# Log sigmoid of the forget gates on GpSimd and ScalarE, places of their own for the extra tokens' values and the last probabilities

## The chip, the core and the metric

The kernel runs on one core of one Trainium2 chip. The time is that of one execution on the device in microseconds (us), median of several runs. The engines are named as the profile names them: PE is TensorE's matmul, PEld its weight load, DVE VectorE, ACT ScalarE, POOL GpSimd, SP the engine that issues the transfers (DMAs).

## What is computed

The reference is one layer of a hybrid decoder: 2048 prompt tokens and 16 meta tokens ahead of them, and 8 samples of 4 tokens that decode from caches. Every token is normalised and projected by one wide matrix; half of the width goes through an mLSTM with four heads, the other half through attention over a window of 128 tokens with sinks; both are gated, projected back to 1024 columns and normalised with the residual. What the change touches is the forget gate of the mLSTM:

```python
def mlstm_inputs(mq, mk, mv, mi, mf):
    ...
    log_i = mi.astype(f32)
    log_f = jax.nn.log_sigmoid(mf.astype(f32))

def mlstm_chunk(state, q, k, v, log_i, log_f):
    b = jnp.cumsum(log_f, axis=1)
    dmat = b[:, :, None, :] - b[:, None, :, :] + log_i[:, None, :, :]
    ...
    m_t = jnp.maximum(inter, jnp.max(dmat, axis=2))
    w = jnp.exp(dmat - m_t[:, :, None, :])
    qk = jnp.einsum('btsh,bshd->btsh', q, k) * w
```

The log sigmoid of f is min(f, 0) - log(1 + e), with e = exp(-|f|). The kernel takes the logarithm as 2 artanh(z) with z = e / (2 + e), by an odd polynomial in z up to z to the 13th.

## The kernel before

The prompt is cut into 16 chunks of 128 tokens, a token to a partition. Matrices are multiplied as two halves of 16 bits each (high and low), so that a projection of 512 columns takes 24 matmuls (`proj`, L298 to L301).

**Start (to about 90 us).** Weights come in pieces, are scaled and split (`prep`, L244 to L277: maxima of the arrived pieces at L261, the split on ACT at L259 and DVE at L276). The 48 extra tokens (32 of the samples, 16 meta tokens) and chunk 0 are projected as the weights come; matmuls at L307 and L308 are those of the extra tokens (tile `px`, evicted at L310 on ACT and at L311 and L317 on DVE). The extra tokens' gates (`ge`, L571) and those of chunk 0 (`gts`, L508) each call `log_sigmoid_rows`; PE transposes the result of the first at L574 and L575. Their values `ve` are written by L317 into the first 48 rows of `vaug[1]` (L546). There are two such buffers, `vaug[0]` and `vaug[1]`: chunk n's values go to `vaug[n % 2]` (L429 and L430), so chunk 1's use the one that holds `ve`. Column 128 of each head in them is 1, written once at the start (L222). Transposed extra tokens (`xef`) lie in the arena `ea`.

**Phase A (to about 515 us).** For each chunk n: the gates (`a_gate`: 16 small matmuls at L513 and L516, the sums on DVE at L518 and L519, then `log_sigmoid_rows` into `Gf[n % 2]`, its forget gates, and `Gi[n % 2]`, its input gates); projections q, k, v and o (evicted by DVE at L433 or L430, two PSUM buffers `pj`; for q and k also L437 on ACT and L438 on DVE); the mLSTM of the chunk, which begins with transposes of Gf and Gi on PE (L749, L750). On POOL run in this phase the products of the queries (L792, behind a transposing DMA into `qT`, and L793) and small powers (L327, L499). Between these steps stand jobs of the samples and the preparation of further weights. The log sigmoid is a chain of small operations of 4 elements a partition in the tile `ls`: 13 on DVE from L472 to L483 with ACT's exponential (L473) among them, and a copy of the input gates (L484), which hangs on nothing else of the chain. It runs 17 times: for the extra tokens and for 16 chunks.

**Phase B (from about 515 us).** For each chunk the attention: projections, then four units of two heads (`s_unit`, L1256: scores on PE at L1271, maxima on DVE at L1272, exponentials on ACT at L1278, the probabilities split into the two halves of `hl` by ACT at L1279 and DVE at L1280, for the meta tokens into `mhl` by ACT at L1283 and POOL at L1284). Units 0 and 1 share one tile `hl`, units 2 and 3 the next; there is one buffer of it, and a transposing DMA reads each pair into a tile from `stg`. The meta tokens' part is transposed in `s_sums` (`mT`), and PE multiplies probabilities and values in `s_pv` (L1313 for meta tokens, L1324 for the window). The output projection is at L1351, and the layer norm follows (on DVE, and on POOL at L340, L1181 and L1182). The last chunk, 15, is written out by hand at the end of the program.

**Order.** The steps are written one after the other in the program, and the framework's scheduler puts each engine's instructions into an order of its own, by its estimate of when each is ready. In that order each engine then works strictly. All transfers are issued by SP, in the order of its queue.

Of the kernel before, what the change touches and what calls it, by code (L numbers as in the profile page):

```python
# [9 lines left out]
F16 = mybir.dt.float16  # L10
BF16 = mybir.dt.bfloat16
I32 = mybir.dt.int32
AF = mybir.ActivationFunctionType
ALU = mybir.AluOpType
AX = mybir.AxisListType

P = 128
D = 1024
KT = 8
NCH = 16  # L20
NM = 16
NS = 32
NE = NS + NM
H = 4
# [17 lines left out]
def tile_hymba_step(  # L42
# [7 lines left out]
    V, A, G, T, S = nc.vector, nc.scalar, nc.gpsimd, nc.tensor, nc.sync  # L50
# [4 lines left out]
    mn = ctx.enter_context(tc.tile_pool(name="mn", bufs=1))  # L55
# [9 lines left out]
    def pt(shape):  # L65
        return psum("pt", shape, 3)
# [7 lines left out]
    def small(tag, n, dt=F32, bufs=2):  # L74
        return sp.tile([P, n], dt, tag=tag, name=tag, bufs=bufs)
# [5 lines left out]
    def work(tag, shape, dt=F32, bufs=None):  # L81
        return mn.tile(shape, dt, tag=tag, name=tag, bufs=bufs or KB4.get(tag, 1))
# [23 lines left out]
    def dmat(out, in_):  # L106
        return dma(out, in_, S.dma_start_transpose)
# [107 lines left out]
    Gi = [cst.tile([P, P], F32, name=f"Gi{i}") for i in range(2)]  # L215
    vaug = [cst.tile([P, H, 129], F32, name=f"vaug{i}") for i in range(2)]
# [250 lines left out]
    def log_sigmoid_rows(gts, rows, buf):  # L467

        f = gts[:, 4:8]
        w = small("ls", 32)[:rows]  # L470
        na, e, d, r, z, z2, q = (w[:, 4 * i:4 * i + 4] for i in range(7))
        V.scalar_tensor_tensor(na, f, -1.0, f, op0=ALU.mult, op1=ALU.min)  # L472
        A.activation(e, na, AF.Exp)  # L473
        V.tensor_scalar(d, e, 2.0, None, op0=ALU.add)
        V.reciprocal(r, d)
        V.tensor_tensor(z, e, r, op=ALU.mult)
        V.tensor_tensor(z2, z, z, op=ALU.mult)
        V.tensor_scalar(q, z2, 1.0 / 13, None, op0=ALU.mult)
        for c in (11, 9, 7, 5, 3):
            V.scalar_tensor_tensor(q, q, 1.0 / c, z2, op0=ALU.add, op1=ALU.mult)  # L480
        V.scalar_tensor_tensor(q, q, 1.0, z, op0=ALU.add, op1=ALU.mult)
        V.tensor_scalar(d, f, 0.0, None, op0=ALU.min)
        V.scalar_tensor_tensor(Gf[buf][:rows, 0:P:32], q, -2.0, d, op0=ALU.mult, op1=ALU.add)  # L483
        V.tensor_copy(Gi[buf][:rows, 0:P:32], gts[:, 0:4])  # L484

    def head_stats(g, nh, dd, rows):

# [14 lines left out]
    def a_gate(n):  # L502
        c = ca[n]
        gts = small("gts", 8)
        if n == 0:
            ps = po([P, 8])
            proj32(ps, lambda k: tg[:, k])
            V.tensor_tensor(gts, ps, bg, op=ALU.add)  # L508
            log_sigmoid_rows(gts, P, 0)
            return  # L510
        ps = pt([P, 16])
        for k in range(KT):
            T.matmul(ps, c.xT[:, k, :], wg.t[:, k].rearrange("p c n -> p (c n)"), start=(k == 0), stop=False,  # L513
                     skip_group_check=True)
        for k in range(KT):
            T.matmul(ps[:, 0:8], c.xT[:, KT + k, :], wg.t[:, k, 0], start=False, stop=(k == KT - 1),  # L516
                     skip_group_check=True)
        V.scalar_tensor_tensor(gts, ps[:, 8:16], wg.ev, bg, op0=ALU.mult, op1=ALU.add)  # L518
        V.scalar_tensor_tensor(gts, ps[:, 0:8], wg.ev, gts, op0=ALU.mult, op1=ALU.add)  # L519
        log_sigmoid_rows(gts, P, n % 2)  # L520
# [15 lines left out]
    def e_arena():  # L536
        return Arena(mn.tile([P, 2048], F32, tag="wkv", name="ea"))

    E = St()
    ea = e_arena()  # L540
# [2 lines left out]
    qe = work("qs", [P, 512])[:NE]  # L543
    ke = work("At", [P, 512])[:NE]
    oe = work("g", [P, 512])[:NE]
    ve = vaug[1][:NE]  # L546

    sto = stage(512, "w")
    load(sto, w_a[3])
# [9 lines left out]
    hl = work("hl", [P, 2, D], F16)  # L559
    ln0_(xe, NE, hl.rearrange("p c d -> p (c d)").bitcast(BF16)[:NE])  # L560
    split_e(EE[:, 0], xe, NE, s_x)
    dmat(ET, EE[:, 0])
    xef = ea.take(8 * NE).rearrange("p (k t) -> p k t", t=NE)
    ps = pt([P, 8, NE])
    for j in range(8):
        T.transpose(ps[:, j], xe[:, j * P:(j + 1) * P], ident[:NE, :NE])
# [2 lines left out]
    for k in range(KT):  # L569
        T.matmul(ps[:NE], xef[:, k], tg[:, k], start=(k == 0), stop=(k == KT - 1))  # L570
    V.tensor_tensor(ge, ps[:NE], bg[:NE], op=ALU.add)  # L571
    log_sigmoid_rows(ge, NE, 1)
    pr = pt([P, 2, P])
    T.transpose(pr[:, 0, :NE], Gf[1][:NE, :], ident[:NE, :NE])  # L574
# [3 lines left out]
    rows = ea.take(3 * NE).rearrange("p (c t) -> p c t", t=NE)  # L578
# [27 lines left out]
                    op=ALU.subtract)  # L606
# [40 lines left out]
    for j in range(2):  # L647
        ps = po([P, 2, 256])
        for i in range(2):
            h = 2 * j + i  # L650
# [605 lines left out]
    def s_unit(n, u):  # L1256

        c = cb[n]
        pvc = cb.get(n - 1)
        lo = 0 if pvc is not None else P  # L1260
        if u % 2 == 0:
            c.hl = work("hl", [P, 2, 4, 256], F16)
        hl, q, h0 = c.hl, u % 2, 2 * u
        mxs, nb, sums = c.mxs, c.nb, c.sums
        mask = swamask[:, c.half, lo:]
        p = work(("g", "SI")[u % 2], [P, 2, NW])
        for i in range(2):
            h = h0 + i
            ps = pt([P, NW])
            for x in range(2):  # L1270
                T.matmul(ps[:, lo:], c.qT[:, h], kTs[:, 2 * (h // 4) + x, lo:], start=(x == 0), stop=(x == 1))  # L1271
            V.tensor_tensor_reduce(p[:, i, lo:], ps[:, lo:], mask, sc_s, sink60[:, h:h + 1],  # L1272
                                   op0=ALU.add, op1=ALU.max, accum_out=mxs[:, h:h + 1])
        hs = slice(h0, h0 + 2)
        V.tensor_scalar(nb[:, hs], mxs[:, hs], -1.0, LN2x12, op0=ALU.mult, op1=ALU.add)  # L1275
        for i in range(2):
            h = h0 + i
            A.activation(p[:, i, lo:], p[:, i, lo:], AF.Exp, bias=nb[:, h:h + 1], accum_out=sums[:, h:h + 1])  # L1278
        A.activation(hl[:, 0, 2 * q:2 * q + 2, lo:], p[:, :, lo:2 * P], AF.Copy)  # L1279
        V.tensor_tensor(hl[:, 1, 2 * q:2 * q + 2, lo:], p[:, :, lo:2 * P], hl[:, 0, 2 * q:2 * q + 2, lo:],  # L1280
                        op=ALU.subtract)
        m = c.mhl[:, u // 2, :, 2 * q:2 * q + 2]
        A.activation(m[:, 0], p[:, :, 2 * P:], AF.Copy)  # L1283
        G.tensor_tensor(m[:, 1], p[:, :, 2 * P:], m[:, 0], op=ALU.subtract)  # L1284
        if lo:
            G.memset(hl[:, :, 2 * q:2 * q + 2, 0:P], 0.0)
        if q:
            pT = work("stg", [P, 2, 4, 2, P], F16)
            dmat(out=pT.rearrange("p c h e q -> p (c h e) q"),
                                  in_=hl.rearrange("p c h k -> p (c h k)"))  # L1290
            c.PT.append(pT)
# [88 lines left out]
    for n in range(NCH - 1):  # L1380
        b_load(n + 1)
        b_q(n)
        b_kv(n)
        if n > 0:
            s_pv(n - 1)
        b_az(n)
        if n == 2:
            b_out(0)
        s_start(n)
        s_unit(n, 0)  # L1390
        s_unit(n, 1)
        b_z(n)
        s_unit(n, 2)
        s_unit(n, 3)
        s_sums(n)
        if n == 0:
            z = work("xs", [P, D])[:NS]
            dma(z, ze_d)
            final(z, NS, y_s)
        elif 1 < n < NCH - 2:  # L1400
            b_out(n - 1)
            cb.pop(n - 2, None)

    n = NCH - 1
# [113 lines left out]
```

## Time and profile before

| | before |
|---|---|
| median of 3 runs | 1063.71 us (1061.87 to 1066.89) |
| profiled execution | 1059.23 us |
| its span on the core | 1057.4 us |
| granted TensorE clock, mean | 0.993 |
| PE busy | 1026.1 us, 97% of the span |
| DVE busy | 728.7 us, 69% |
| ACT busy | 441.3 us, 42% |
| POOL busy | 247.6 us, 23%, 270 instructions |

The page gives busy time by engine, then the span in 40 slices (a digit is the busy share in tenths; PEclk is the clock that TensorE was granted), then the chain of work that ended last. A row of a timeline reads: start, duration, engine, line, operation, what is written from what, with the shape, how often, and in brackets the idle time of the engine before it and what ended that. A row of the waits of an engine reads: the instruction's line, what it waited for, total us, how many times, the longest.

### The profile page before, as it was taken

What the parts mean: (1) busy time and instruction counts of PE and PEld (TensorE: products, weight loads), DVE (VectorE), ACT (ScalarE), POOL (GpSimd) and SP (SyncE); (2) the same over time, 40 slices, a digit from 0 to 9 for tenths busy, and PEclk for the clock granted to TensorE, in tenths of its full rate; (3) what the DMA queues carried; (4) which work ended last, traced back from release to release, by engine and by line L of the source; (5) the groups of instructions that cost most, each with busy time, mean ns of one, the idle gap of its engine ahead of it and who ended that gap; (6) DMA issues with size and microseconds to landing.
All of it is one profiled execution on the core that took longest, in us unless ns stands there. A gap on an engine that the chain in (4) does not pass through costs nothing.

```text
span 1057.4 us, 17650 instructions
## 1 busy us (share of the span) xinstructions
PE 1026.1 (97%) x6399; PEld 571.0 (54%) x6399; DVE 728.7 (69%) x2056; ACT 441.3 (42%) x1112; POOL 247.6 (23%) x270
## 2 busy tenths in 40 slices
PE   7998999999999999999999999999999999999996
PEld 3544666655556555555565555555555455555552
DVE  5996876767766887787557676656566566666674
ACT  5783333336244554552334334343334333343430
POOL 2101313211111001013111332233331233332322
PEclk9998999999999999999999999999999999999998
DMA  9946366464794775755866463555445555545452
GB/s 332 267 133 164 99 145 154 115 187 88 233 236 123 222 247 140 231 133 160 291 188 124 92 160 89 132 131 117 108 113 127 128 124 139 108 102 135 113 114 76
DMA packets 245809, 161.83 MB, mean 153 GB/s; under 512 B 207945, under 2 KB 220953, under 8 KB 244409
## 3 DMA queue, kind: packets, MB, share of 16 engines
q1 hardware_dynamic: 245722, 160.70, 58.3%
q8 instruction: 50, 0.82, 0.3%
q14 instruction: 37, 0.30, 0.1%
HBM read 68.22 MB, written 43.58 MB: 106 GB/s over the span
## 4 chain that ended last, share of the span: by engine, by line
PE 69%; DMA 11%; DVE 10%; ACT 6%; issue 3%; POOL 1%; SPq 1%; DVEq 0%; ACTq 0%
PE pj L1351 14%; PE pj L301 14%; PE pj L298 14%; PE pj L299 14%; DMA stg<-hl 3%; PE pt L1271 3%; PE po L1324 2%; DMA stg<-in_dram 1%; DMA xT<-hl 1%; DMA kT<-kh 1%; ACT w_o L259 1%; DMA wd_o<-w_o 1%; DVE w_o L276 1%; PE po L816 1%; PE po L817 1%
## 5 line engine op out<-in xcount | busy, mean ns | idle before, releaser
L301 PEld LDWEIGHTS <-xT 128*128 128x128 f16 x992 | 96.9, 98 | 98.2 <-issue 1.0
L299 PEld LDWEIGHTS <-xT 128*128 128x128 f16 x992 | 97.4, 98 | 96.7 <-issue 5.2
L298 PEld LDWEIGHTS <-xT 128*128 128x128 f16 x992 | 97.4, 98 | 94.1 <-issue 2.8
L1351 PEld LDWEIGHTS <-EE 128*128 128x128 f16 x720 | 70.3, 98 | 79.0
L1351 PE MATMUL pj<-wr_o,EE 128*128 128x512 f16 x360 | 82.3, 379 | 0.0
L1351 PE MATMUL pj<-w_o,EE 128*128 128x512 f16 x360 | 82.1, 379 | 0.0
L1278 ACT ACTIVATE SI<-SI,nb 128x272 f32<-128x272 f32 (+1 forms) x64 | 32.4, 507 | 66.0 <-DVE nb L1275 66.0
L298 PE MATMUL pj<-w_o,xT 128*128 128x512 f16 x120 | 46.9, 390 | 3.2 <-DVE vaug L430 3.2
L1278 ACT ACTIVATE g<-g,nb 128x272 f32<-128x272 f32 (+1 forms) x64 | 32.2, 503 | 42.4 <-DVE nb L1275 42.4
L1284 POOL TENSOR_TENSOR mhl<-SI,mhl 128x32 f16<-128x32 f32 x32 | 12.6, 395 | 157.6 <-ACT mhl L1283 157.6
L298 PE MATMUL pj<-wr_az,xT 128*128 128x512 f16 x128 | 48.5, 379 | 0.0
L299 PE MATMUL pj<-wr_z,xT 128*128 128x512 f16 x128 | 48.5, 379 | 0.0
L298 PE MATMUL pj<-wr_aq,xT 128*128 128x512 f16 x128 | 48.5, 379 | 0.0
L299 PE MATMUL pj<-wr_aq,xT 128*128 128x512 f16 x128 | 48.5, 379 | 0.0
L299 PE MATMUL pj<-wr_az,xT 128*128 128x512 f16 x128 | 48.5, 379 | 0.0
L298 PE MATMUL pj<-wr_z,xT 128*128 128x512 f16 x128 | 48.5, 379 | 0.0
L793 POOL TENSOR_TENSOR qs<-qs,SI 128x512 f32<-128x512 f32 x16 | 20.9, 1307 | 113.5 <-ACT SI L784 113.3
L299 PE MATMUL pj<-w_o,xT 128*128 128x512 f16 x120 | 46.7, 390 | 0.0
L1181 POOL TENSOR_TENSOR xs<-xs,gb 128x1024 f32<-128x1024 f32 (+1 forms) x16 | 42.8, 2674 | 15.4 <-DMA stg<-hl 9.3
L298 PE MATMUL pj<-w_v,xT 128*128 128x512 f16 x120 | 46.0, 383 | 0.0
L299 PE MATMUL pj<-w_v,xT 128*128 128x512 f16 x120 | 45.8, 382 | 0.0
L792 POOL TENSOR_TENSOR qs<-qT 128x512 f32<-128x512 f16 x16 | 20.2, 1260 | 109.2 <-DMA qT<-qh 58.9
(463 smaller groups left out, 2492.1 us busy)
## 6 DMA issues: line engine op xcount, KB each, us to landing
stg<-in_dram SPq DMA_DIRECT2D x28, 512.0 KB
xs<-in_dram SPq DMA_DIRECT2D x16, 512.0 KB
h_d<-xs SPq DMA_DIRECT2D x16, 512.0 KB
xT_d<-xT SPq DMA_DIRECT2D x16, 512.0 KB
xs<-h_d SPq DMA_DIRECT2D x16, 512.0 KB
xT<-xT_d SPq DMA_DIRECT2D x16, 512.0 KB
out_dram<-xs SPq DMA_DIRECT2D x15, 512.0 KB
hn_d<-g SPq DMA_DIRECT2D x16, 258.0 KB
```

What stands on the lines that cost most here:

```text
L259: A.activation(w.t[:, 2 * i:2 * i + 2, 0, :], s, AF.Abs, accum_out=mx4[:, i:i + 1])
L298: T.matmul(ps, xT[:, k, :], w.t[:, k, 0, :n], start=(k == 0), stop=False)
L299: T.matmul(ps, xT[:, k, :], w.t[:, k, 1, :n], start=False, stop=False)
L301: T.matmul(ps, xT[:, KT + k, :], w.t[:, k, 0, :n], start=False, stop=(k == KT - 1))
L792: G.tensor_tensor(c.qs, c.qT[:, 0], c.qT[:, 1], op=ALU.add)
L793: G.tensor_tensor(c.qs, c.qs, c.SI, op=ALU.mult)
L1181: G.tensor_tensor(z, z, lg[:rows], op=ALU.mult)
L1271: T.matmul(ps[:, lo:], c.qT[:, h], kTs[:, 2 * (h // 4) + x, lo:], start=(x == 0), stop=(x == 1))
L1278: A.activation(p[:, i, lo:], p[:, i, lo:], AF.Exp, bias=nb[:, h:h + 1], accum_out=sums[:, h:h + 1])
L1284: G.tensor_tensor(m[:, 1], p[:, :, 2 * P:], m[:, 0], op=ALU.subtract)
L1324: T.matmul(pso[:, h], l, r, start=False, stop=(i == len(last) - 1), skip_group_check=True)
L1351: T.matmul(ps, c.yT[:, a, :], w[:, k, t, :], start=(first and j == 0), stop=(last and j == len(mm) - 1))
```

## The change

Three things.

- `log_sigmoid_rows`: the exponent's argument is now |f|, by ACT's Abs, and the exponential takes it with scale -1. Of the thirteen DVE operations two stay there, the reciprocal and the last combination into Gf; the others run on POOL, as products and sums apart (a step of the polynomial that was one operation of DVE is two of POOL), and min(f, 0) is now half of f - |f|. With the copy of the input gates POOL has 18 operations in a call. The polynomial is the same.
- The extra tokens' values `ve` get a place of their own in the arena `ea`, with their ones column written there; to make room, `xef` moves to a tile `kw`.
- In chunk 15 the units 2 and 3 write their probabilities into a tile of their own, `hl2`, in the buffer that held the weights `wkv`.

Lines shift: what is L484 to L545 in the kernel before is 3 lines further down in the changed one, L546 to L1261 is 4 further, and what follows L1262 is 7 further.

```diff
@@ -469,19 +469,22 @@
         f = gts[:, 4:8]
         w = small("ls", 32)[:rows]
         na, e, d, r, z, z2, q = (w[:, 4 * i:4 * i + 4] for i in range(7))
-        V.scalar_tensor_tensor(na, f, -1.0, f, op0=ALU.mult, op1=ALU.min)
-        A.activation(e, na, AF.Exp)
-        V.tensor_scalar(d, e, 2.0, None, op0=ALU.add)
+
+        A.activation(na, f, AF.Abs)
+        A.activation(e, na, AF.Exp, scale=-1.0)
+        G.tensor_scalar(d, e, 2.0, None, op0=ALU.add)
         V.reciprocal(r, d)
-        V.tensor_tensor(z, e, r, op=ALU.mult)
-        V.tensor_tensor(z2, z, z, op=ALU.mult)
-        V.tensor_scalar(q, z2, 1.0 / 13, None, op0=ALU.mult)
-        for c in (11, 9, 7, 5, 3):
-            V.scalar_tensor_tensor(q, q, 1.0 / c, z2, op0=ALU.add, op1=ALU.mult)
-        V.scalar_tensor_tensor(q, q, 1.0, z, op0=ALU.add, op1=ALU.mult)
-        V.tensor_scalar(d, f, 0.0, None, op0=ALU.min)
+        G.tensor_tensor(z, e, r, op=ALU.mult)
+        G.tensor_tensor(z2, z, z, op=ALU.mult)
+        G.tensor_scalar(q, z2, 1.0 / 13, 1.0 / 11, op0=ALU.mult, op1=ALU.add)
+        for c in (9, 7, 5, 3, 1):
+            G.tensor_tensor(q, q, z2, op=ALU.mult)
+            G.tensor_scalar(q, q, 1.0 / c, None, op0=ALU.add)
+        G.tensor_tensor(q, q, z, op=ALU.mult)
+        G.tensor_tensor(d, f, na, op=ALU.subtract)
+        G.tensor_scalar(d, d, 0.5, None, op0=ALU.mult)
         V.scalar_tensor_tensor(Gf[buf][:rows, 0:P:32], q, -2.0, d, op0=ALU.mult, op1=ALU.add)
-        V.tensor_copy(Gi[buf][:rows, 0:P:32], gts[:, 0:4])
+        G.tensor_copy(Gi[buf][:rows, 0:P:32], gts[:, 0:4])
 
     def head_stats(g, nh, dd, rows):
 
@@ -543,7 +546,8 @@
     qe = work("qs", [P, 512])[:NE]
     ke = work("At", [P, 512])[:NE]
     oe = work("g", [P, 512])[:NE]
-    ve = vaug[1][:NE]
+    ve = ea.take(H * 129).rearrange("p (h d) -> p h d", d=129)[:NE]
+    G.memset(ve[:, :, 128:129], 1.0)
 
     sto = stage(512, "w")
     load(sto, w_a[3])
@@ -560,7 +564,7 @@
     ln0_(xe, NE, hl.rearrange("p c d -> p (c d)").bitcast(BF16)[:NE])
     split_e(EE[:, 0], xe, NE, s_x)
     dmat(ET, EE[:, 0])
-    xef = ea.take(8 * NE).rearrange("p (k t) -> p k t", t=NE)
+    xef = work("kw", [P, 512])[:, 0:8 * NE].rearrange("p (k t) -> p k t", t=NE)
     ps = pt([P, 8, NE])
     for j in range(8):
         T.transpose(ps[:, j], xe[:, j * P:(j + 1) * P], ident[:NE, :NE])
@@ -1259,7 +1263,10 @@
         pvc = cb.get(n - 1)
         lo = 0 if pvc is not None else P
         if u % 2 == 0:
-            c.hl = work("hl", [P, 2, 4, 256], F16)
+            if n == NCH - 1 and u == 2:
+                c.hl = mn.tile([P, 2, 4, 256], F16, tag="wkv", name="hl2")
+            else:
+                c.hl = work("hl", [P, 2, 4, 256], F16)
         hl, q, h0 = c.hl, u % 2, 2 * u
         mxs, nb, sums = c.mxs, c.nb, c.sums
         mask = swamask[:, c.half, lo:]
```

Where instructions move, at three places. First DVE at the start, where the two chains of the extra tokens (48 rows, `Gf_121`) and of chunk 0 (128 rows, `Gf_120`) end. `L480` and `L481` are steps of the polynomial, `L433 o` is an eviction of a projection, `L438` the low half of chunk 0's keys. Before:

```order
L433 SCALAR_TENSOR_TENSOR o<-pj,bias 128x512
L480 SCALAR_TENSOR_TENSOR ls<-ls 48x4
L124 TENSOR_SCALAR cols<-cols 128x1
L480 SCALAR_TENSOR_TENSOR ls<-ls 128x4
L265 TENSOR_REDUCE mx<-mx_621 128x1
L481 SCALAR_TENSOR_TENSOR ls<-ls 48x4
L126 TENSOR_SCALAR cols<-cols 128x1
L481 SCALAR_TENSOR_TENSOR ls<-ls 128x4
L135 TENSOR_SCALAR dg<-cs,mx 128x128
L483 SCALAR_TENSOR_TENSOR Gf_121<-ls 48x4
L270 TENSOR_SCALAR cols<-cols 128x1
L483 SCALAR_TENSOR_TENSOR Gf_120<-ls 128x4
```

After:

```order
L276 SCALAR_TENSOR_TENSOR w_k<-stage,cols,w_k 128x2x512
L438 SCALAR_TENSOR_TENSOR kh<-k,cols,kh 128x512
L486 SCALAR_TENSOR_TENSOR Gf_121<-ls 48x4
L486 SCALAR_TENSOR_TENSOR Gf_120<-ls 128x4
L381 SCALAR_TENSOR_TENSOR xs<-xs,lns,gb 128x1024
L137 TENSOR_REDUCE cols<-po 128x1
L122 TENSOR_SCALAR cols<-cols 128x1
L124 TENSOR_SCALAR cols<-cols 128x1
L126 TENSOR_SCALAR cols<-cols 128x1
L270 TENSOR_SCALAR cols<-cols 128x1
L433 SCALAR_TENSOR_TENSOR o<-pj,bias 128x512
```

The steps of the polynomial are gone from DVE, and the two last rows, which now wait for POOL (L486), stand next to each other, ahead of the layer norm L381 and the eviction of o instead of behind them.

POOL has these operations of both calls in alternation (the 48 rows, then the 128), with the product of chunk 0's queries (L796, before L792) ahead of the last 14 of them. The transposes of the extra tokens' gates on PE, which wait for the first of DVE's two last rows, stand at another place as well. `px<-w_k` is the projection of the extra tokens' keys, `pj<-w_q` that of chunk 1's queries. Before:

```order
L298 LDWEIGHTS xT
L298 MATMUL pj<-w_q,xT 128x512
L136 MATMUL po<-dg,ones 128x128
L574 MATMUL pt<-cs,Gf_121 128x48
L575 MATMUL pt<-cs,Gi_123 128x48
L299 LDWEIGHTS xT
L299 MATMUL pj<-w_q,xT 128x512
```

After:

```order
L307 LDWEIGHTS EE
L307 MATMUL px<-w_k,EE 128x512
L578 MATMUL pt<-cs,Gf_121 128x48
L579 MATMUL pt<-cs,Gi_123 128x48
L308 LDWEIGHTS EE
L308 MATMUL px<-w_k,EE 128x512
```

They stood near the end of the queries' 24 matmuls and stand now ahead of the last five matmuls of the extra tokens' keys, which come before the queries.

The third place is DVE where chunk 1's values are evicted into `vaug_125` (L430). `L261` are maxima of arriving weights, L696 (now L700, in the changed order just ahead of the rows shown) a copy of an arriving piece of a sample's state. Before:

```order
L644 TENSOR_SCALAR kw<-At,ea 48x128 x4
L696 COPY da<-ea 128x8
L261 TENSOR_REDUCE mx_1803<-stg 128x1 x2
L311 TENSOR_TENSOR g<-g,bias 48x512
L261 TENSOR_REDUCE mx_1803<-stg 128x1
L317 SCALAR_TENSOR_TENSOR g<-px,cols,g 48x512
L430 SCALAR_TENSOR_TENSOR vaug_125<-pj,cols,bias 128x4x128
L261 TENSOR_REDUCE mx_1803<-stg 128x1
```

After:

```order
L762 SCALAR_TENSOR_TENSOR r_726<-fi,cols,rb 128x128
L763 SCALAR_TENSOR_TENSOR rM<-r_726,cols,rb 128x128
L398 SCALAR_TENSOR_TENSOR hl<-xs,cols,hl 128x1024
L648 TENSOR_SCALAR kw<-At,ea 48x128 x4
L430 SCALAR_TENSOR_TENSOR vaug_125<-pj,cols,bias 128x4x128
L311 TENSOR_TENSOR g<-g,bias 48x512
L782 TENSOR_TENSOR ws<-am,pt 128x4
L786 SCALAR_TENSOR_TENSOR wt<-pt,am,cs 128x128 x2
L317 SCALAR_TENSOR_TENSOR g<-px,cols,g 48x512
L786 SCALAR_TENSOR_TENSOR wt<-pt,am,cs 128x128 x2
L261 TENSOR_REDUCE mx_1835<-stg 128x1 x4
L433 SCALAR_TENSOR_TENSOR k<-pj,cols,bias 128x512
```

The eviction of the values stands ahead of all four maxima; behind them the next eviction, that of k (L433), follows.

In the tail the rows of PE are the same. On DVE and ACT the halves of `hl2` stand earlier than those of `hl` did, on DVE the first half ahead of the eviction of the keys (L1227, now L1231); on SP the transposing DMA of `hl2` is issued right behind that of `mhl` and ahead of the load of xs, which it followed before.

## Prediction

> **What bounds the kernel now.** I read the page first: busy time, the slices, and the shares of the chain that ended last.
>
> ```profile
> PE 1026.1 (97%) x6399; PEld 571.0 (54%) x6399; DVE 728.7 (69%) x2056; ACT 441.3 (42%) x1112; POOL 247.6 (23%) x270
> ...
> PE   7998999999999999999999999999999999999996
> ...
> PEclk9998999999999999999999999999999999999998
> ...
> PE 69%; DMA 11%; DVE 10%; ACT 6%; issue 3%; POOL 1%; SPq 1%; DVEq 0%; ACTq 0%
> ```
>
> TensorE is busy for 97% of the span. What is moved from DVE to POOL can therefore pay only where TensorE waits for DVE. Next I read the waits of TensorE by line, and in the chain of waits one stretch of its plain work.
>
> ```profile
> PE po L1324 <- DMA stg<-hl: 5.1, 5, 2.1
> PE pj L298 <- DVE vaug L430: 3.2, 1, 3.2
> PE pt L749 <- DVE Gf L483: 2.9, 2, 1.7
> PE pt L612 <- ACT ea L607: 1.1, 1, 1.1
> ```
>
> ```profile
> 592.50 5.18 PE pj L1351 x24
> ```
>
> One matmul of 512 columns takes 5.18 / 24 = 0.216 us. The change can touch these waits: the 3.2 us for the values of chunk 1, the 2.9 us for the forget gates (two chunks of sixteen), part of the 1.1 us at L612 and the last of the waits at L1324. Together that is about 9 of 1059 us. The busy time by stretch and the timeline of TensorE show one more cost beside the largest wait.
>
> ```profile
> 50.00:75.00 25.00, 25.00 (x107) 11.55 (x107) 24.66 (x63) 24.03 (x37) 3.15 (x3) 1.00 0.56 168
> 75.00:100.00 25.00, 20.61 (x122) 11.00 (x120) 18.52 (x49) 8.24 (x25) 3.56 (x4) 0.86 0.51 127
> ```
>
> ```profile
> 91.77 0.58 PE L298 MATMUL pj<-w_o,xT 128*128 128x512 f16 x1 [3.19 <-DVE vaug L430]
> 92.15 0.63 PE L299 MATMUL pj<-w_o,xT 128*128 128x512 f16 x1
> 92.58 0.63 PE L298 MATMUL pj<-w_o,xT 128*128 128x512 f16 x1
> ...
> 96.33 0.38 PE L299 MATMUL pj<-w_o,xT 128*128 128x512 f16 x1
> ```
>
> (The columns of the stretches: busy us of PE, PEld, DVE, ACT and POOL, then the granted clock.) After the idle 3.19 us the matmuls start 0.43 us apart instead of 0.216, and the stretch's clock is 0.86. Ten of them come that slowly before they are short again at 96.33, so the idle time costs 10 x 0.21 = 2.1 us on top. The Trainium skill, "TensorE: Matmul & The Clock Gate", Part 1, has the clock halve after an idle window of about 3.4 us; here a gap of 3.19 us sufficed. The first of these stretches also shows DVE full (24.66 of 25), which matters below.
>
> **Values in a place of their own.** Why the values of chunk 1 are late is read from DVE's timeline.
>
> ```profile
> 83.15 0.87 DVE L644 TENSOR_SCALAR kw<-At,ea 48x128 f32<-48x128 f32 x4
> 85.54 0.17 DVE L696 COPY da<-ea 128x8 f32<-128x8 f32 x1 [1.53 <-DMA da<-in_dram]
> 87.72 1.50 DVE L261 TENSOR_REDUCE mx<-stg 128x1 f32<-128x512 f32 x2 [2.00 <-DMA stg<-in_dram]
> ...
> 89.73 0.67 DVE L261 TENSOR_REDUCE mx<-stg 128x1 f32<-128x512 f32 x1
> 90.33 0.73 DVE L317 SCALAR_TENSOR_TENSOR g<-px,cols,g 48x512 f32<-48x512 f32 x1
> 90.99 0.73 DVE L430 SCALAR_TENSOR_TENSOR vaug<-pj,cols,bias 128x512 f32<-128x512 f32 x1
> ```
>
> L430 stands behind maxima (L261) that wait for weights from DRAM. It could not stand earlier, since the extra tokens' values sat in its buffer. In the changed order it stands ahead of all four L261, with about 2.6 us of other rows between the copy at 85.54 and it (two small rows of a few tenths, L398 of the size of an L276, 1.27 us by the row further down, and the four L644, now L648, 0.87 in all). That puts its end near 88.8 us, and TensorE asks for it at 91.77 - 3.19 = 88.58. So 0.2 us of the 3.19 is left, the clock stays up, and the gain is 3.0 + 2.1 = 5.1 us. Next in danger is the eviction of k (L433), now behind the four L261. It would begin near 91 us, when TensorE still has 24 x 0.216 = 5.2 us of the o projection ahead of it. I charge 0.3 us for that, with bounds 0 and 1: net -4.8 us, -5.1 to -4.1.
>
> **The log sigmoid, at the start.** Before, DVE worked the two chains (48 and 128 rows) between other work; after, DVE keeps the reciprocal and the last row of each, and POOL does eighteen operations per call, the two calls alternating. Before, the reciprocals ran at 47.09 and the last rows at 59.2.
>
> ```profile
> 47.09 0.22 DVE L475 RECIPROCAL ls<-ls 48x4 f32<-48x4 f32 x2
> ...
> 47.81 1.27 DVE L276 SCALAR_TENSOR_TENSOR w_k<-stage,cols,w_k 128x1024 f16<-128x1024 f32 x1
> ...
> 59.14 0.15 DVE L483 SCALAR_TENSOR_TENSOR Gf<-ls 48x4 f32<-48x4 f32 x1
> ```
>
> ```profile
> 58.00 0.38 PE L308 MATMUL px<-w_k,EE 128*128 128x512 f16 x1
> ...
> 62.63 0.26 PE L574 MATMUL pt<-cs,Gf 48*128 48x48 f32 x1
> ```
>
> No row has such an operation on POOL. The nearest are these, by line (duration in ns: min/median/max), and the group of the large product.
>
> ```profile
> L1284 POOL TENSOR_TENSOR mhl<-SI,mhl x32: 243/246/783, 554.4 to 1025.6; 128x32 f16<-128x32 f32 x32
> L327 POOL TENSOR_TENSOR lns<-lns,mhalf x16: 548/1151/2422, 21.8 to 452.0; 128x1 f32<-128x1 f32 x15, 48x1 f32<-48x1 f32 x1
> L793 POOL TENSOR_TENSOR qs<-qs,SI 128x512 f32<-128x512 f32 x16 | 20.9, 1307 | 113.5 <-ACT SI L784 113.3
> ```
>
> From 32 to 512 elements a row the time grows by (1307 - 246) / 480 = 2.2 ns an element, so four elements take 246 - 28 x 2.2 = 184 ns; with a hop to the next, dependent one I take 0.25 us. The bounds are 0.18 (no hop) and 0.55 (the shortest L327, one element, another function).
>
> ```profile
> 51.29 1.60 POOL L792 TENSOR_TENSOR qs<-qT 128x512 f32<-128x512 f16 x1 [12.89 <-DMA e_d<-qs]
> ```
>
> Between the reciprocals and the last rows POOL has 32 of these operations and this product of chunk 0's queries (L796 after): 47.3 + 32 x 0.25 + 1.6 = 56.9 us. At 0.18 it would be 54.7, at 0.55 66.5. TensorE's transposes of the gates have moved ahead too: they stood at 62.63 and stand now five matmuls ahead of the end of w_k's, at 58.00 in the time of before. Undisturbed they would just not wait. But the DVE rows in between are four L276 of 1.27 us and one L438, all with two inputs in SBUF, and with such rows POOL does collide:
>
> ```profile
> 484.63 0.23 DVE L519 SCALAR_TENSOR_TENSOR gts<-pt,cols,gts 128x8 f32<-128x8 f32 x1
> ...
> 486.69 1.60 DVE L476 TENSOR_TENSOR ls<-ls 128x4 f32<-128x4 f32 x1
> ...
> 488.52 2.21 DVE L478 TENSOR_SCALAR ls<-ls 128x4 f32<-128x4 f32 x1
> ...
> 493.45 0.17 DVE L483 SCALAR_TENSOR_TENSOR Gf<-ls 128x4 f32<-128x4 f32 x1
> ```
>
> ```profile
> 485.92 2.35 POOL L1181 TENSOR_TENSOR xs<-xs,gb 32x1024 f32<-32x1024 f32 x1 [1.52 <-DVE ls L474]
> 488.35 2.35 POOL L1182 TENSOR_TENSOR xs<-xs,gb 32x1024 f32<-32x1024 f32 x1
> ```
>
> Two four-element rows of DVE, of a kind that lasts 0.17 at 493.45, end at 488.29 and 490.73, with POOL's two products (488.27 and 490.70). The Trainium skill, "SBUF — State Buffer", section "Who interferes with whom", says it as a rule: a DVE operation with two SBUF inputs and a GpSimd one that reads SBUF share a port, and the second to issue is blocked to the end of the first; the trace agrees in the 1.60 us. By that rule alone, every DVE row above could hold POOL's chain for its whole length.
>
> In this case's rows the worst at the start is 4 x 1.27 + 0.74 = 5.8 us: 56.9 + 5.8 = 62.7, a wait of 4.7 us at 58.00, and DVE itself stands at the last row meanwhile, with the eviction of o behind it. A wait that long would bring the slow clock again (2.1 us). I take the middle, about +2.0 us; bounds 0 and +6.8.
>
> **The log sigmoid, in chunks 1 to 15.** DVE loses thirteen rows a chunk and gains none; at 0.15 us that is 13 x 15 x 0.15 = 29 us, but beside a TensorE that is full, so its worth is only the waits that DVE causes: the 2.9 us at L749. The new chain has fifteen dependent operations on POOL, so 15 x 0.25 = 3.8 us, two on ScalarE and two on DVE with their hops (about 1.2 us) and 0.5 us to evict the gates: 5.5 us undisturbed. Before, from L519 to L483, it took 493.45 - 484.63 = 8.8 us in the chunk above, where POOL's two products were in the way; such products now stand in POOL's own queue, ahead of or between the chain's operations. TensorE's cover between the gates' matmuls and their transposes is by the order 24 to 67 matmuls before (5.2 to 14.5 us) and 35 to 77 after (7.6 to 16.6 us). So an undisturbed chain is covered, and one that meets a product of 1.3 us and some blocked ports (7 to 10 us) is not, in the four or five chunks with 35 to 38 matmuls. DVE's last row (L486) then also holds the evictions behind it. I weigh a gain of 2 (most of the 2.9) against five chunks that wait 0.6 each: net +1.0, with bounds -2.9 and +9 (fifteen chunks at 0.6).
>
> ScalarE gains one Abs a chunk; it is at 42% and I cost that at nothing. The memset of the ones column is done at the start, while POOL has nothing else, and x1's transposed copy in the kw tile stands where nothing else needs it yet: nothing.
>
> **The last probabilities.** With a second hl tile in chunk 15 the two last units need not wait until the transposing DMA has read the first.
>
> ```profile
> 1025.46 0.63 ACT L1279 ACTIVATE hl<-g 128x512 f16<-128x512 f32 x1
> ...
> 1027.34 0.68 DVE L1280 TENSOR_TENSOR hl<-SI,hl 128x512 f16<-128x512 f32 x1
> ...
> 1028.08 3.17 SPq L104 DMA_TRANSPOSE stg<-hl  x1
> ...
> 1033.33 0.87 PE L1324 MATMUL po<-vd,stg 128*128 128x64 f16 x24 [2.14 <-DMA stg<-hl]
> ```
>
> The issue at 1028.08 waits for the last half of hl; in the new order it stands right behind the transposition of mhl, ahead of the load of xs, and could come at about 1027.1, as DVE's last half no longer stands behind other rows. Against that, 0.68 us of DVE (the first half) now stands ahead of the eviction of the keys and the maxima, on the same path. So -1.0 + 0.7 = -0.3 us, with bounds -1.3 and +2 (the half blocked by a POOL product of 2.35 us). The output projection after it stays as it is.
>
> **The sum,** against the profiled execution's 1059.23 us (span 1057.4 and 1.8 around it): -4.8 + 2.0 + 1.0 - 0.3 = -2.1, so 1057.1. The profiled run is 4.5 us under the median of the three runs, 1063.71; carried over, the forecast is 1063.71 - 2.1 = 1061.6 us. A measurement of this kernel tells some 0.5% (5.3 us) from no change; the forecast is inside that.
>
> **Rivals.** *All of it comes through.* The chains stay under their cover, DVE is lighter by 29 us, and the waits at L430 with their slow clock (5.1), L749 (2.9), L612 (half, 0.5) go: -8.5 with nothing given back, 1055.2. For it: TensorE asks for DVE's results in few places, and the start has DVE at 24.66 of 25. Against: POOL's small operations are long beside DVE's. Chance 0.32.
>
> *POOL's chain becomes what TensorE waits for.* Place: the transposes at L753. Price: at 0.45 us an operation the chain is 15 x 0.45 + 1.7 = 8.5 us and some 2 us of blocked ports beside it, which passes the cover of 7.6 us in five chunks and holds DVE's evictions in the rest; 2.5 x 5 + 0.3 x 10 = 15 less the 4.8 of the values is about +10, 1073.9; with 0.35 us an operation it is +6, 1069.7. It decides from about 0.35 us an operation, beyond my 0.25 and inside the bounds. For it: L327 lasts 1.15 at the median against 0.55 undisturbed. The Trainium skill, "Perfetto Trace Analysis", section "Optimizing Scalar/DVE Operations", also warns that moving work between these two engines might not help, for the same shared port; no run here shows that yet. Chance 0.25.
>
> *The wait only moves.* TensorE waits 4.7 us for the gates at the start, with the slow clock there instead of at 91: -4.8 + 6.8 + 1.0 - 0.3 = +2.7, 1066.4. For it: DVE is full there, and both ends of the chain were drawn closer. Chance 0.15; the forecast itself has 0.28.
>
> **How the numbers follow.** Faster by over 0.5% is the first rival, 0.32; slower by over 0.5% the second, 0.25; the forecast and the moved wait lie within, 0.43. The range takes in the first rival with the gain of the tail (-1.3) and 2 us for its unknowns, down to 1052, and the second up to its middle, 1072.
>
> **What would show it.** Right: no wait at L298 for L430 and full clock from 75 to 100 us; DVE's busy time down by about 30 us and POOL's up by 17 x 18 x 0.2 = 61; POOL's operations start 0.2 to 0.3 us apart; TensorE waits at L578 by under 4 us, and at L753 in a few chunks by under 1 us; the last wait at L1324 near 1.8. Wrong: operations over 0.35 us apart, waits at L753 in most chunks, DVE idle ahead of L486 with evictions behind it, or a new wait at L298 for L433.

## The result, and the profile after

The changed kernel takes 1076.09 us (median of 3 runs, 1074.83 to 1077.24) against 1063.71: a ratio of 1.0113 with a 95% interval of 1.0087 to 1.0138. It is slower by about 12 us, beyond the upper end of the range (1072). The profiled execution took 1077.24 us with a span of 1075.4. Single executions of one program differ by some us (23 runs of the kernel before, taken beside the experiments, went from 1057.55 to 1067.71), so ratios below come from the timed runs, and the profiles say where, not how much to the last us.

The page after, in the parts that answer to those of before:

```profile
PE 1031.6 (96%) x6399; PEld 572.3 (53%) x6399; DVE 701.1 (65%) x1835; ACT 442.4 (41%) x1129; POOL 333.5 (31%) x577
...
PEclk9998999999999999999999999999999999999999
...
PE 61%; DMA 15%; DVE 9%; POOL 5%; ACT 5%; issue 3%; SPq 1%; DVEq 0%; ACTq 0%; POOLq 0%
```

DVE lost 27.6 us of busy time and POOL gained 85.9, and POOL now holds 5% of the chain that ended last, where it held 1%. Where in the run the time went is read from the busy times of two stretches, the first half and the rest, after and then before (columns as in the prediction):

```profile
0.00:515.00 515.00, 482.97 (x2808) 272.70 (x2809) 349.45 (x846) 234.03 (x508) 168.84 (x380) 0.98 0.63 173
```

```profile
0.00:515.00 515.00, 496.68 (x2936) 283.00 (x2937) 385.44 (x1095) 238.34 (x507) 88.65 (x92) 0.99 0.65 180
```

In the first 515 us TensorE is 128 instructions behind, and nothing is added later: the scores of the first attention chunk start 19 us later in this pair of profiles, those of the last 18.5. The whole loss is in phase A and the start. The waits of TensorE in the changed kernel that differ most from before (the one at L1331 was larger before, 5.1 in all with a longest of 2.1; the others were smaller or not there):

```profile
PE px L307 <- DVE ea L317: 4.9, 1, 4.9
PE px L703 <- DMA da<-e_d: 4.4, 2, 3.4
PE pt L753 <- DVE Gf L486: 4.2, 2, 3.4
PE po L1331 <- DMA stg<-hl: 3.5, 5, 1.7
PE pt L807 <- ACT w_aq L259: 2.5, 1, 2.5
PE pt L516 <- ACT am L777: 2.2, 1, 2.2
PE pj L298 <- DVE o L433: 1.4, 1, 1.4
```

The wait for L430 is gone, but one of 4.9 us for L317 has taken its place, with the slow clock behind it. Between 100 and 515 us TensorE's waits come to some 17 us, where they were 6. Those for the gates (L753) are only 4.2 of them, 1.3 more than before; the rest of the increase stands at other rows (L703, L807, L298). The waits of DVE name what DVE stands for now:

```profile
DVE Gf L486 <- POOL ls L483: 24.0, 14, 4.4
```

In 14 of 17 calls DVE stands at the last row of the log sigmoid until POOL is done, 24 us in all. How far apart POOL's operations stand, undisturbed, is read from its timeline in the last chunk; the rows are start, duration, engine, line:

```profile
529.50 0.20 POOL L481 TENSOR_TENSOR ls<-ls 128x4 f32<-128x4 f32 x1
529.78 0.22 POOL L482 TENSOR_SCALAR ls<-ls 128x4 f32<-128x4 f32 x1
530.09 0.20 POOL L481 TENSOR_TENSOR ls<-ls 128x4 f32<-128x4 f32 x1
```

Dependent operations stand 0.28 to 0.31 us apart. A chunk where it goes wrong is the one whose gates are evicted at 371.88 to 372.11. Here are ACT, POOL, DVE and TensorE in it:

```profile
374.30 1.06 ACT L323 ACTIVATE hl<-xs 128x1024 bf16<-128x1024 f32 x1 [3.18 <-DMA xT<-hl]
...
376.86 0.19 ACT L473 ACTIVATE ls<-gts 128x4 f32<-128x4 f32 x1
```

```profile
377.36 1.34 POOL L327 TENSOR_TENSOR lns<-lns,mhalf 128x1 f32<-128x1 f32 x1 [5.00 <-ACT lns L326]
378.68 0.22 POOL L475 TENSOR_SCALAR ls<-ls 128x4 f32<-128x4 f32 x1
379.50 1.14 POOL L477 TENSOR_TENSOR ls<-ls 128x4 f32<-128x4 f32 x1 [0.59 <-DVE ls L476]
...
382.31 1.25 POOL L482 TENSOR_SCALAR ls<-ls 128x4 f32<-128x4 f32 x1
383.65 1.22 POOL L481 TENSOR_TENSOR ls<-ls 128x4 f32<-128x4 f32 x1
...
387.03 0.20 POOL L483 TENSOR_TENSOR ls<-ls 128x4 f32<-128x4 f32 x1
387.18 1.15 POOL L796 TENSOR_TENSOR qs<-qT 128x512 f32<-128x512 f16 x1
```

```profile
379.33 1.26 DVE L382 SCALAR_TENSOR_TENSOR xs<-xs,lns,gb 128x1024 f32<-128x1024 f32 x1
...
382.20 1.28 DVE L398 SCALAR_TENSOR_TENSOR hl<-xs,cols,hl 128x1024 f16<-128x1024 f32 x1
...
383.53 1.28 DVE L276 SCALAR_TENSOR_TENSOR w_z<-stg,cols,w_z 128x1024 f16<-128x1024 f32 x1
...
387.26 1.09 DVE L486 SCALAR_TENSOR_TENSOR Gf<-ls 128x4 f32<-128x4 f32 x1 [2.45 <-POOL ls L483]
```

```profile
388.40 0.48 PE L753 MATMUL pt<-cs,Gf 128*128 128x128 f32 x1 [3.36 <-DVE Gf L486]
```

Four things stretch the chain to 16.2 us from the gates to Gf. The chain's first step stands behind the layer norm of another chunk on ACT, which waits for a transfer (4.8 us to 376.86). Its first operation on POOL stands behind L327 of the same layer norm (1.3). Three operations on POOL last 1.14 to 1.25 instead of 0.2 and end with a two-input row of DVE (380.64 and 380.59; 383.56 and 383.48; 384.87 and 384.81). And DVE's last row in its turn lasts 1.09 and ends with POOL's product (388.35 and 388.33). Over the fifteen chunks the time from the end of L522 to that of L486 is 9.3 us in the mean (5.6 to 16.2); from L519 to L483 it was 6.8 before (2.8 to 11.2).

### The profile page after: what moved, and what is told of

Same layout as the page of the kernel before. It is cut to its first block, busy times and chain, and to the rows that moved or that the text cites. A ratio compares the mean times of both kernels' runs of the same rounds, so it can differ in the third digit from the quotient of the medians.

```text
span 1075.4 us, 17718 instructions
## 1 busy us (share of the span) xinstructions
PE 1031.6 (96%) x6399; PEld 572.3 (53%) x6399; DVE 701.1 (65%) x1835; ACT 442.4 (41%) x1129; POOL 333.5 (31%) x577
## 4 chain that ended last, share of the span: by engine, by line
PE 61%; DMA 15%; DVE 9%; POOL 5%; ACT 5%; issue 3%; SPq 1%; DVEq 0%; ACTq 0%; POOLq 0%
PE pj L1358 14%; PE pj L301 12%; PE pj L299 11%; PE pj L298 11%; DMA xT<-hl 3%; PE pt L1278 2%; DMA stg<-hl 2%; PE po L1331 2%; POOL ls L482 1%; PE pj L417 1%; SPq L104 1%; POOL ls L481 1%; DMA stg<-in_dram 1%; DMA da<-e_d 1%; DMA wd_z<-w_z 1%
## 5 line engine op out<-in xcount | busy, mean ns | idle before, releaser
L298 PEld LDWEIGHTS <-xT 128*128 128x128 f16 x992 | 97.6, 98 | 94.2 <-issue 1.7
L298 PE MATMUL pj<-wr_az,xT 128*128 128x512 f16 x128 | 48.5, 379 | 0.0
L298 PE MATMUL pj<-wr_aq,xT 128*128 128x512 f16 x128 | 48.5, 379 | 0.0
L298 PE MATMUL pj<-wr_z,xT 128*128 128x512 f16 x128 | 48.5, 379 | 0.0
L298 PE MATMUL pj<-w_k,xT 128*128 128x512 f16 x120 | 45.5, 379 | 1.4 <-DVE o L433 1.4
L298 PE MATMUL pj<-w_q,xT 128*128 128x512 f16 x120 | 46.5, 387 | 0.0
L299 PE MATMUL pj<-w_q,xT 128*128 128x512 f16 x120 | 46.4, 387 | 0.0
L298 PE MATMUL pj<-w_v,xT 128*128 128x512 f16 x120 | 45.5, 379 | 0.8 <-DVE q L433 0.8
L1291 POOL TENSOR_TENSOR mhl<-g,mhl 128x32 f16<-128x32 f32 x32 | 19.4, 606 | 85.9 <-ACT mhl L1290 81.5
```

Source lines behind the costliest of these rows:

```text
L298: T.matmul(ps, xT[:, k, :], w.t[:, k, 0, :n], start=(k == 0), stop=False)
L299: T.matmul(ps, xT[:, k, :], w.t[:, k, 1, :n], start=False, stop=False)
```

## The experiments

**The parts by themselves.** Theory A held that the log sigmoid on POOL costs the time and the values' place gains; theory B that any change of the scheduler's order in the first half costs. Each of the first three kernels has one part of the change (the diff's hunk), e4 has two; the rest is as before.

```diff
 e1: the hunk of log_sigmoid_rows alone
 e2: the hunks of ve and xef alone
 e3: the hunk of hl2 alone
 e4: ve, xef and hl2, log sigmoid on DVE
```

> Only the log sigmoid moved to POOL and ACT; values and last probabilities as before. Theory A (the chain on POOL, with the order that it brings, costs the time; the two places by themselves gain): slower than before by 12 to 20 us, so at 1.012 to 1.019, with DVE idle 4 us at its last row at the start (L486 of the change), waits of PE for Gf of 3 us or more in all, and the wait for the values of chunk 1 (3 us) still there in some form. Theory B (any change of the order of the first half costs, through waits at the scarce buffers; POOL itself is not the cause): slower by 5 to 10 us only, the rest coming from the values' place. If the order of ratios is that this one is faster than before, both are wrong.

Measured: 1.0147 (1.0120 to 1.0173), 1079.24 us. That is inside theory A's span and above theory B's. Beside the whole change (1.0113) the intervals overlap.

> Only the extra tokens' values and xef in places of their own; the log sigmoid on DVE. By its order DVE takes L317 into the arena and L430 of chunk 1 ahead of the copies that wait for the samples' state. Theory A: faster than before by 4 to 5 us (0.995 to 0.996), no wait of PE for the values near 88 us nor for L317, clock 1.00 from 75 to 100 us. Theory B: the order differs from before in 1386 matmul places, so slower by 3 to 8 us, from waits elsewhere in the first half.

Measured: 1.0060 (1.0039 to 1.0082). Theory A is wrong here: slower by some 6 us, as theory B had it. Its waits of TensorE:

```profile
PE pt L804 <- DMA kT<-kh: 3.3, 1, 3.3
PE px L700 <- DMA da<-e_d: 2.9, 1, 2.9
PE pt L769 <- DVE rM L760: 2.2, 1, 2.2
```

The wait for the values is gone, and others stand in its place, none of which was over 0.3 us before, for transfers and rows that the new order asks for earlier than they come.

> Only the last probabilities in a buffer of their own. PE's order is that of before throughout. Both theories: within 1 us of before; the last wait at L1324 shrinks from 2.1 us to between 1.2 and 2.0 us. In the changed kernel it was 1.7.

Measured: 0.9976 (0.9959 to 0.9992), with a last wait at L1324's counterpart of 1.7 us. The gain of 2.5 us is more than the 1 us that both theories allowed, though the interval comes down to 0.9 us.

> Both places, the log sigmoid on DVE as before: the change without its first part. Theory A: faster than before by 4.5 to 6 us (0.994 to 0.996), the sum of the two runs with one part each; and so the log sigmoid alone costs 15 us or more. Theory B: slower than before by 3 to 8 us, as with the values alone.

Measured: 1.0053 (1.0028 to 1.0078). Again theory B's side. So neither theory holds for all four kernels, and the parts do not add: each edit has an order of its own.

**The order and the operations apart.** For this the kernels tie each engine's instructions to a given order, read from the other build, by edges that order the issue and wait for nothing; only the operations that differ find their places freely. So the log sigmoid's place (DVE or POOL) and the order of all else (before's or the change's) make four cases (edits shortened).

```diff
 f1: after.py, and at the end of tile_hymba_step
+    for e, seq in order_of_before:
+        for a, b in zip(seq, seq[1:]):
+            tc.add_manual_dep(mine[b], mine[a].name, NoSync)
 f2: before.py, the same with the order of after
 f3: e4 with the order of before; on DVE, L430 of chunk 1 put behind L759
```

> The whole change (log sigmoid on POOL and ACT, both places), but every other instruction of PE, DVE, ACT, POOL and SP is held in the order that it has in the kernel before; only the log sigmoid's own operations and the memset of the ones column find their places freely. Theory O (the order that the scheduler draws for PE, DVE and SP costs the time): between -2 and +4 us of before (0.998 to 1.004). Theory P (the chain on POOL and the wait of DVE for it cost the time, whatever the order): near the changed kernel, +9 to +15 us (1.009 to 1.014), with waits of PE at L749's counterpart for Gf of several us.

Measured: 1.0108 (1.0077 to 1.0140). Theory P. In the order of before, the waits for the gates are the largest term:

```profile
PE pt L758 <- DVE Gf L490: 9.9, 6, 3.6
```

(L758 and L490 are L749 and L483 of before, which had 2.9 us in two chunks.) TensorE's order is the same in both, so its rows can be laid side by side. Here is the longest of these waits in f1 and then the same place in the kernel before, each with a matmul of 512 columns behind it (0.63 us long at the slow clock, 0.38 at the full one):

```profile
503.79 0.45 PE L758 MATMUL pt<-cs,Gf 128*128 128x128 f32 x1 [3.64 <-DVE Gf L490]
...
504.24 0.63 PE L301 MATMUL pj<-w_o,xT 128*128 128x512 f16 x1
```

```profile
493.76 0.30 PE L749 MATMUL pt<-cs,Gf 128*128 128x128 f32 x1 [1.71 <-DVE Gf L483]
...
494.00 0.38 PE L298 MATMUL pj<-w_o,xT 128*128 128x512 f16 x1
```

At 84 us of the kernel before, f1 stands 5.7 us behind it on TensorE, but at 96.5 us only 0.3: the kernel before waits there for the values (L430), f1 hardly does, and so the lateness is swallowed. From there the distance grows to 12.5 us at 496, most of it at the transposes L758 and at the slow matmuls behind two of them (seven of 512 columns behind the wait at 184.75, seven behind the one shown). Neither place can gain much in this order (h2 and f3 below), so f1 measures the log sigmoid.

> The kernel before, log sigmoid on DVE and no new places, but every other instruction held in the order that it has in the changed kernel. Theory O: near the changed kernel, +9 to +15 us (1.009 to 1.014), with waits of PE at the same places: px for L317 near 87 us, da<-e_d near 165, L753's and L807's counterparts. Theory P: near before, within 3 us, since nothing of the chain is on POOL.

Measured: 1.0234 (1.0199 to 1.0270), slower than both theories said. The waits that theory O named are there: 4.7 us for L317's counterpart, 3.4 for da<-e_d, 8.3 for Gf in one chunk, 1.2 at L807's counterpart. The order of the change, drawn up for a log sigmoid on POOL, suits the one on DVE worse than either kernel's own. f2 also lacks the two new places, so it differs from the changed kernel in more than the log sigmoid.

| log sigmoid on | order of before | order of the change |
|---|---|---|
| DVE | 1 | 1.0234 |
| POOL | 1.0108 | 1.0113 |

So the operations on POOL cost 1.1% with the order of before held. In the order of the change the same comparison goes the other way (1.0234 against 1.0113). The two effects do not add, and the table does not say how the loss of the changed kernel divides between them. The order by itself can cost as much as the operations and more.

> Both places, log sigmoid on DVE, all in the order of the kernel before but for one row: the eviction of chunk 1's values goes up on DVE to right behind the rows of the scans, ahead of the copies and maxima that wait for transfers (one more row trades places with a neighbour). Theory O: faster than before by 4 to 6 us (0.994 to 0.996), which is the term of 4.8 us that the prediction gave to the values' place, plus some tenths of hl2; no wait for the values near 88 us and clock 1.00 from 75 to 100 us. Under the rival that such a gain is always lost at the next DMA wait (da<-e_d near 95 us, as in the run with the values alone), within 2 us of before.

Measured: 0.9976 (0.9956 to 0.9997). Its profile has no wait for the values, and the gates of chunk 2 come 3.9 us earlier than in the profile of before; the tail kept the old order of SP in this run, so hl2 could not act. By the ratio the gain is 2.6 us, between what theory O and its rival had. In the profile 2.2 us of the 3.9 go again near 491 us, in a longer wait for Gf (2.5 us against 1.7) and slow matmuls behind it.

**What about the chain costs.** Three kernels on f1, each with the order of before (edits shortened).

```diff
 g1: -        for c in (9, 7, 5, 3, 1):
     +        for c in (1,):
 g2: -        V.scalar_tensor_tensor(Gf..., q, -2.0, d, mult, add)
     +        G.tensor_scalar(q, q, -2.0, None, op0=ALU.mult)
     +        G.tensor_tensor(Gf..., q, d, op=ALU.add)
 g3: the calls for the extra tokens and chunk 0 with the DVE body of before
```

> As f1 (the whole change in the order of before), but four of the five steps of the polynomial are left out, so POOL's chain has eight operations fewer, about 2.4 us at the 0.3 us that dependent ones stand apart. What is left out are terms of the logarithm. f1 stood at 1.011. Theory C (TensorE waits for the end of the chain): the waits for Gf fall from 9.9 us to 2 to 5 us and the time to 1.002 to 1.006 of before. If the cost is not the chain's length but that DVE stands at its last row or shares a port with POOL, still 1.008 to 1.011.

Measured: 1.0003 (0.9981 to 1.0025). The waits for Gf:

```profile
PE pt L758 <- DVE Gf L490: 4.0, 1, 4.0
```

Eight operations fewer, and the whole loss is gone: theory C, a little beyond its own figure. From the gates to Gf it is 5.7 us in the mean here, and 9.0 in f1. The shorter chain also lets DVE stand less at its last row (18.1 us, 26.1 in f1); the next kernel takes that apart.

> As f1, but the last combination into Gf is made on POOL too (two operations in place of DVE's one), so that DVE never stands waiting for POOL's chain but at the reciprocal. DVE's idle time of 26 us at that row goes. Theory C (TensorE waits for the end of the chain): the chain is some 0.3 us longer, the waits for Gf stay at 8 to 12 us, the time at 1.008 to 1.012. Theory D (DVE, stopped at the last row, is late with evictions and splits for which TensorE waits): 1.001 to 1.005, and the waits at the samples' rows (L616's counterpart, 2.5 us) shrink.

Measured: 1.0109 (1.0076 to 1.0143). DVE never stands at the last row, and nothing is won. TensorE waits for the chain that now ends on POOL:

```profile
PE pt L759 <- POOL Gf L491: 17.1, 7, 5.0
```

So the 26 us that DVE stands at that row in f1 are not the main cost (theory D falls): TensorE waits for the chain's end itself. The 17.1 us are more than the 8 to 12 expected, but the profiled execution is the slowest of this kernel's four (1082.70 us) and that of f1 the fastest of its six (1070.90), so the two totals cannot be set against each other. A smaller cost of DVE's standing could hide behind the longer waits.

> As f1, but the two calls at the start (extra tokens and chunk 0) stay on DVE as before; chunks 1 to 15 are on POOL. If the start has a share (DVE stands 4 us at its last row near 55 to 59 us, and the values' eviction and the slow clock follow), the time falls by 3 to 5 us against f1, to 1.006 to 1.008. If the start's lateness is anyhow absorbed by the wait for the values near 88 us, it stays at 1.010 to 1.012.

Measured: 1.0077 (1.0048 to 1.0107). By the ratios the start's share is 0.3%, some 3 us, and the fifteen chunks have about 8 (5 to 11). But the intervals of f1 and g3 overlap, and f1's profile shows the rival of this expectation: the lateness at the start is swallowed by the wait for the values, down to 0.3 us. So the start's share is not shown.

**The rest.**

```diff
 h1: e4 with the order of e3, L430 of chunk 1 behind L759 as in f3
 h2: e2 with the order of before
```

> Both places and the log sigmoid on DVE; all in the order of the kernel before, but for the values' eviction one place up (as f3) and the tail's rows as in the run with hl2 alone. In f3 the tail kept the old order of SP, so that hl2 could not act there; f3 and hl2 alone each stood at 0.9976. If the two gains add: 0.995 to 0.9965, 1058 to 1060 us, the fastest of these. If f3's gain near 88 us is swallowed later in the first half by the wait for Gf near 491 us, as its profile shows for 2.2 of 3.7 us: 0.9965 to 0.998.

Measured: 0.9977 (0.9959 to 0.9995). The two gains do not add by what can be measured. It is as fast as e3 and f3 and faster than both kernels of this case.

> Only the values' place (as the run with the values alone, which stood at 1.006), but all in the order of the kernel before. If the order that the scheduler drew cost that run its 0.6%: 0.998 to 1.002, with the wait for the values near 88 us as before. If the place itself costs (another memory place, one memset more): 1.004 to 1.008.

Measured: 1.0008 (0.9990 to 1.0027). The place itself costs nothing that can be measured, and the wait for the values is there as before (2.7 us); the 0.6% of e2 are the order's.

## Why the prediction was wrong

**Values in a place of their own: -4.8 forecast, not had.** The step said that L430 would be done near 88.8 us with TensorE asking at 88.58. L430 did run at 89.50, ahead of the maxima, as the order said. It ended at 90.24, 1.4 us later than the step said, since the copy ahead of it (86.91) came later. But TensorE had stopped earlier, at another row of the same queue:

```profile
81.91 1.28 DVE L382 SCALAR_TENSOR_TENSOR xs<-xs,lns,gb 128x1024 f32<-128x1024 f32 x1 [0.44 <-POOL lns L327]
83.12 0.68 DVE L311 TENSOR_TENSOR g<-g,bias 48x512 f32<-48x512 f32 x1
85.14 0.18 DVE L700 COPY da<-ea 128x8 f32<-128x8 f32 x1 [1.35 <-DMA da<-in_dram]
...
86.00 0.73 DVE L317 SCALAR_TENSOR_TENSOR ea<-px,cols,g 48x512 f32<-48x512 f32 x1
```

```profile
86.79 0.61 PE L307 MATMUL px<-w_o,EE 128*128 128x512 f16 x1 [4.85 <-DVE ea L317]
87.19 0.63 PE L308 MATMUL px<-w_o,EE 128*128 128x512 f16 x1
87.62 0.63 PE L307 MATMUL px<-w_o,EE 128*128 128x512 f16 x1
```

The eviction of the extra tokens' values (L317) now stands behind a copy that waits 1.35 us for a transfer (L700), where it stood ahead of it; L382 and L311 are also in front of it. `px` has one buffer, so the next projection of the extra tokens waits for it. f2, in the same order but without the new place, has this wait too (4.7 us): it comes with the order. I followed the one row that the change was about and not every eviction ahead of it in the new order. The price of the wait was near: f3, which moves that row alone, gains 5.5 us there (5.1 in the sum), of which 1.9 go in the next wait, for a transfer (da<-e_d) and not for the eviction of k. That the wait only moves was a rival, but I had it move to the gates at the start, where TensorE waited 0.53 us.

**The log sigmoid at the start: +2.0 forecast, not shown.** DVE stood 4.4 us at L486 (59.53), as the rows allowed. f1 against g3 gives 1.0108 - 1.0077, 3.3 us, within the bounds, but with overlapping intervals, and in f1's profile 0.3 us are left after the wait for the values. In the changed kernel's own order this share was not separated.

**The log sigmoid in chunks 1 to 15: +1.0 forecast, about 8 in the order of before.** This is the step that failed: a gain of 2 us, most of the 2.9 at L749, weighed against five chunks that wait 0.6 us each. By g3 the fifteen chunks on POOL cost 0.77%, 8 us, just inside the bound of 9 that I gave and did not weigh. In f1's profile six chunks wait, 1.65 us each in the mean and 9.9 in all, where before there were 2.9; so nothing was gained and 7 us lost. Some 3 us more are the 14 slow matmuls behind two of the waits (14 x 0.21), which the sum charged at the start alone.

What made the waits so long? The chain undisturbed is 5.6 us in the shortest chunk, against my 5.0 without the gates' eviction, and operations stand 0.29 us apart, against 0.25. Two things were wrong. The mean chain is 9.3 us, 2.5 more than before; between its shortest case (5.6) and that mean lie the queues of ACT and POOL and the blocked ports, and I had taken the disturbed chain for the exception. And I laid the cover of 7.6 to 16.6 us against the chain with 0.5 us to evict the gates; but the second row of that eviction starts 3.0 us in the mean after the last gate matmul in the profile after (0.3 to 10.1), as it did before (3.6). The time that the chain needs is therefore 12.5 us in the mean in the changed kernel and 12.3 in f1, against 10.7 before, and TensorE's own work up to the transposes lasts 8.8 to 17.2 us in f1. g1 shows that the length decides: with eight operations less the loss is gone.

In the changed kernel itself, in its own order, this cover lasts 9.6 to 18.9 us, and only two chunks wait (4.2 us). There much of the loss has moved to rows that the new order puts elsewhere, and its division was not separated. The second rival's place was right in the order of before (the transposes at L753); its condition, 0.35 us an operation, was not, since it happens at 0.29. That its total, +10, lies near the measured +12 is partly luck: it put the chain at 15 us and took 4.8 off for the values, where the runs show about 8 and nothing.

The rule of the Trainium skill in "Perfetto Trace Analysis", section "Optimizing Scalar/DVE Operations", that work moved between DVE and GpSimd might not help, held here: DVE was busy 27.6 us less, and that bought no time. The shared port, which that section gives as the reason, is a part of it and not the whole: the rows of the chunk at 371.88 show blocked operations in both directions, and f1's cost goes with the chain's length. How much would be left without blocked ports was not separated.

**The last probabilities: -0.3 forecast, -2.5 measured** (0.9976, that is -0.9 to -4.4 us). Right in sign; the last wait fell from 2.1 to 1.7 us, 0.4 where the sum had 0.3, and the rows do not show where the rest comes from. h1, which adds the same rows to f3, is no faster than f3.

**The sum.** The two parts of the change that touch phase A were each costed at the rows of before, with the order changing only at the places looked at. The order of the change puts 2077 of TensorE's 5956 instructions at another place than before, and e2 and f2 show that such a new order can cost 0.6 to 2.3%. Beyond the three places looked at, that term was put at nothing in the sum, without a reason.

## What to carry to other kernels

When operations leave a busy engine that nothing waits for, the question is not what that engine gains but how long the chain becomes for the engine that waits at its end. Add the queueing ahead of its first step, count dependent operations at their start-to-start time, and hold that against the cover. Where a scheduler draws the order, a small edit redraws it everywhere; look through the new order for every row that stands behind a wait for a transfer, and separate order from operations by holding one of them fixed. Here only kernels that left the log sigmoid on DVE and nearly all of the order as it was were faster than before, by 0.2%.

## What the runs showed of the hardware

- A wait shorter than the 3.19 us of the prediction can bring the slow clock too. In the changed kernel TensorE waited 2.5 us until 243.7 us and about six matmuls behind it stood 0.43 us apart; before, a wait of 1.83 us until 395.29 was followed by seven of them from 396.9 on, while one of 1.71 us until 493.76 was followed by none. The Trainium skill, "TensorE: Matmul & The Clock Gate", Part 1, has an idle window of about 3.4 us.
- An undisturbed POOL operation of four elements a partition lasts 0.20 us (two tensors) or 0.22 (a scalar); independent ones start 0.15 to 0.2 us apart, dependent ones 0.28 to 0.31; on DVE, in the kernel before, five dependent steps of the polynomial took 0.93 us together (at 492.28), 0.19 each.
